# The down projection of twelve inner tiles as a 2x2 block product, with its operands formed in the gate and up phase

## The chip, the cores and the metric

The kernel runs on one core of a Trainium2 chip. That core has a matrix engine (TensorE, PE in the profile), a vector engine (VectorE, DVE), a scalar engine (ScalarE, ACT), GpSimd (POOL), and SyncE (SP), whose queue issues all transfers of this kernel. The metric is the device time of one execution in microseconds.

## The reference

One encoder layer on 1024 tokens of width 1024, in float32: a feed-forward half step, a mixer, a second feed-forward half step, each followed by a layer norm.

```python
def swiglu_ffn(x, w_gate, w_up, w_down):
    return (jax.nn.silu(x @ w_gate) * (x @ w_up)) @ w_down
...
    x = layer_norm(ALPHA * x + 0.5 * swiglu_ffn(x, ffn1_w_gate[l], ffn1_w_up[l], ffn1_w_down[l]), ln1_g[l], ln1_b[l])
    x = layer_norm(ALPHA * x + hybrid_mixer(x, w_in[l], na_rpb[l], ...), ln2_g[l], ln2_b[l])
    x = layer_norm(ALPHA * x + 0.5 * swiglu_ffn(x, ffn2_w_gate[l], ffn2_w_up[l], ffn2_w_down[l]), ln3_g[l], ln3_b[l])
```

The inner width of the feed-forward is 2816 = 22 tiles of 128. The mixer is not touched by the change.

## The kernel before

**Layout.** Activations are held transposed: a tile is 128 features by 512 tokens, so an activation of width 1024 is 8 tiles `d` by 2 halves `h` of the tokens. Every float32 matrix product is three passes over a pair of rounded parts: with a = ah + al and b = bh + bl it is ah·bh + ah·bl + al·bh (`mm_steps`, L108). So each tile that feeds a product exists as a pair, high and low, made by `split` (L123): a copy on ScalarE rounds, a subtraction on VectorE leaves the rest. Weights are loaded whole and split the same way in `load_w` (L94).

**Stages of a feed-forward** (class `Ffn`, L412; method `go`, L613). Two inner tiles are formed plainly (`glu`, L448). The other twenty are formed in `blocks` (L511): gate and up of a tile, over the two halves of the input features and the two halves of the tokens, are a 2x2 block product, done in seven products of four feature tiles each instead of eight (Winograd's form of Strassen). `factors` (L472) forms the seven weight factors on VectorE and ScalarE, `sums_of` (L430) the four sums of the input, `product` (L499) runs one product of 12 matmuls. The products of one tile are interleaved with the last two of the tile before: `s3` and `a22` of the previous tile stand between those of the present one. At the end a last round has only those two. Each inner tile is written to DRAM (`hid`, L535 and L550).

Then comes down: `down_block` (L600) reads tiles 0 to 5 and then 6 to 11 back (`fetch`, L592), splits them, and adds their product with the down weights, for each `d` and `h`, into an accumulator `acc[d][h]` (L573) that starts as 2·ALPHA·x + product (L567, L569). The last ten tiles are done half by half (`finish`, L576): all `d` of the first 512 tokens, then all `d` of the second. The layer norm of a half (`Norm`, L197) runs beside the matmuls of what follows. In the second feed-forward the second half is cut into two parts of 256 tokens; the last one is normed token by token (`TokenNorm`, L321) into a different output.

**What sets the order.** PE runs its instructions in the order in which they are written. The other engines and SP's queue get their order from a planner that simulates the program; `high_priority(offset=HOIST)` lets an instruction come up to 100 places early. Within one tag of a pool the slots are handed out in the order of the program. The steps of a norm are placed by a clock of estimated matmul time: `at(delay, fn)` (L176) puts `shift`, `stats`, `scale` and `apply` some units after the step before (`LAGS_A` and the like), one unit being about one microsecond; a `gap` spaces the eight `apply` steps. The transposes and spreading matmuls of the norm stand at those places in PE's order. After the first feed-forward, `tok_major` (L674) is the first reader of the normed activation, first of its first 512 tokens.

**Memory.** `xpool` has 32 slots for the pairs of the current activation, `apool` 16 for the accumulators and residuals, the feed-forward's own pool 14 pairs `hh`/`hl`, four `sr` and seven `hr`, and `wpool` two raw weight buffers and four pairs `wh`/`wl`, open for the whole kernel. PSUM has four banks for products (`dps`, L120).

Of the kernel before, what the change touches and what calls it, by code (L numbers as in the profile page):

```python
# [24 lines left out]
BLOCKS = ((0, 6), (6, 6))  # L25
LAST = ((12, 6), (18, 4))
# [13 lines left out]
LAGS_A = (5.0, 9.5, 8.0, 2.0)  # L40
LAGS_B = (2.6, 5.5, 4.7, 1.3)
# [15 lines left out]
def hybrid_layer(ctx, tc, xT, wg1, wu1, wd1, wg2, wu2, wd2, wcol, wnv, wgv, wdl, wgate,  # L57
# [3 lines left out]
    ln_lags = {(0, 0): (LAGS_A, 2.0), (0, 1): (LAGS_B, 0.0),  # L61
# [13 lines left out]
    wpool = pool(ctx, "wpool", 4)  # L75
# [4 lines left out]
    dram = pool(ctx, "dram", 1, DRAM)  # L80

# [12 lines left out]
    def load_w(src, n, resident=False, ahead=HOIST):  # L94
        raw = wpool.tile([P, n], F32, tag="raw", name=nm("raw"), bufs=2)
        if resident:
            wh, wl = xpool.tile([P, n], F32R, tag="x", name=nm("wh")), \
                xpool.tile([P, n], F32R, tag="x", name=nm("wl"))
        else:
            wh = wpool.tile([P, n], F32R, tag="wh", name=nm("wh"))  # L100
            wl = wpool.tile([P, n], F32R, tag="wl", name=nm("wl"))
# [49 lines left out]
    raw = wpool.tile([P, D], F32, tag="raw", name=nm("raw"), bufs=2)  # L151
    first = [wpool.tile([P, D], F32R, tag=t, name=nm(t)) for t in ("wh", "wl")]
# [259 lines left out]
    class Ffn:  # L412
        def __init__(self, stack, x, xr, hs, wg, wu, wd, idx):
            self.x, self.xr, self.hs, self.wg, self.wu, self.wd = x, xr, hs, wg, wu, wd
            self.idx = idx
            self.hp = pool(stack, "hp", 14)
            self.T = [[None] * 4 for _ in range(4)]
            self.acc = [[None, None] for _ in range(KD)]
            self.ht = [[None, None] for _ in range(FT)]
            self.tmp = tagged(self.hp, ("hr",), 7)  # L420

# [26 lines left out]
        def glu(self, f, ws, h, c0=0, cn=HF, spill=False):  # L448
            cs = slice(c0, c0 + cn)
            rhs = [(a[:, cs], b[:, cs]) for a, b in (self.x[k][h] for k in range(KD))]  # L450
            pg = dps()[:, :cn]
            yield from mm_steps(pg, ws[0], rhs)
            pu = dps()[:, :cn]
            yield from mm_steps(pu, ws[1], rhs)
            with hoist():
                sl = stage()[:, :cn]
                nc.scalar.activation(sl, pg, AF.Silu)
                hr = self.tmp()[:, :cn]
                nc.vector.tensor_tensor(hr, pu, sl, ALU.mult)
            if spill:  # L460
                nc.sync.dma_start(self.hs[f, :, h * HF:(h + 1) * HF], hr)
                return
# [762 lines left out]
```

## Time and profile before

| | us |
|---|---|
| runs: median (lowest to highest) of 3 | 2195.89 (2193.54 to 2195.95) |
| the profiled execution, its own time | 2196.31 |
| its span in the trace | 2194.5 |
| first feed-forward: down starts | 435.6 |
| first feed-forward: last ten tiles, first half | 566.1 to 620.5 |
| first feed-forward: last ten tiles, second half | 620.5 to 685.5 |
| second feed-forward: down starts | 1920.0 |
| second feed-forward: last ten tiles, two parts of the second half | 2105 to 2181 |

A time of a stage is read on PE's timeline, from the span's start. The duration of a matmul in a row is longer than the time it costs, since matmuls overlap; the distance between the starts of two of them is what PE pays. A group of instructions by line can be that of a helper (L115 to L117, L124, L125), so shapes and tile names tell what is meant: `hh`, `hl` are a pair of an inner tile or a factor, `xh`, `xl` of the activation, `wh`, `wl` of weights, `hr` a staging tile, `d` a bank of PSUM.

### The profile page before, as it was taken

Reading aid. Unit: us, or ns where it says so; the run is one execution under the profiler, and the core shown is the slowest. Engines: PE = TensorE matmul, PEld = TensorE weight load, DVE = VectorE, ACT = ScalarE, POOL = GpSimd, SP = SyncE. Lnnn points to the kernel's source line nnn. Section 1 sums busy time; section 2 is a strip of 40 time slices with the busy share of each in tenths; the row PEclk is TensorE's granted clock in tenths of the full one; section 3 lists DMA queues with packets and bytes.
Section 4 is the critical chain, followed back from the end, with each engine's and each line's share of the span. In section 5 each row is a group of like instructions: output and inputs, shape, how many; then the busy total and the mean of one; then the engine's idle time right before and its main releaser. Section 6 shows DMA issues by size and latency. Waiting matters only on the chain.

```text
span 2194.5 us, 26421 instructions
## 1 busy us (share of the span) xinstructions
PE 2155.8 (98%) x10160; PEld 1749.6 (80%) x10160; DVE 1249.0 (57%) x2076; ACT 869.6 (40%) x1379; POOL 99.0 (5%) x96
## 2 busy tenths in 40 slices
PE   9999999999999999999999999999999999999987
PEld 7888888888878867777777788877888888888877
DVE  7655555454567354545667533599755555454467
ACT  6433333321334344446566522245533333322334
POOL 0000000000014000000000000043000000000011
PEclk9999999999999999999999999999999999999989
DMA  5222222333332322223332222321322222333333
GB/s 170 91 85 79 82 87 87 113 117 103 98 94 81 112 77 85 86 70 110 101 92 78 92 78 86 92 86 44 103 80 87 87 86 75 112 121 110 112 112 113
DMA packets 97278, 207.01 MB, mean 94 GB/s; under 512 B 10144, under 2 KB 27296, under 8 KB 97152
## 3 DMA queue, kind: packets, MB, share of 16 engines
q1 hardware_dynamic: 97152, 205.32, 29.4%
q8 instruction: 80, 1.31, 0.2%
q14 instruction: 46, 0.38, 0.1%
HBM read 165.31 MB, written 39.98 MB: 94 GB/s over the span
## 4 chain that ended last, share of the span: by engine, by line
PE 87%; DVE 8%; ACT 2%; issue 1%; DMA 1%; POOL 0%; SPq 0%; DVEq 0%; ACTq 0%
PE d L505 11%; PE d L507 11%; PE d L506 11%; PE d L115 11%; PE d L117 11%; PE d L116 11%; PE d L584 3%; PE d L583 3%; PE d L585 3%; PE d L684 1%; PE d L686 1%; PE d L685 1%; PE po L829 1%; PE pt L811 1%; PE s L794 1%
## 5 line engine op out<-in xcount | busy, mean ns | idle before, releaser
L104 ACT ACTIVATE wh<-raw 128x768 fp32r<-128x768 f32 (+2 forms) x167 | 147.3, 884 | 366.0 <-PE d L116 242.4
L115 PE MATMUL d<-xh,wh 128*128 128x512 f32 x640 | 260.0, 406 | 0.2
L116 PE MATMUL d<-xl,wh 128*128 128x512 f32 x640 | 251.1, 392 | 1.0 <-POOL xl L393 0.5
L117 PE MATMUL d<-xh,wl 128*128 128x512 f32 x640 | 251.2, 392 | 0.5 <-DVE wl L105 0.5
L105 DVE TENSOR_TENSOR wl<-raw,wh 128x768 fp32r<-128x768 f32 (+2 forms) x167 | 170.2, 1021 | 136.3 <-ACT wh L104 135.6
L124 ACT ACTIVATE hh<-sr 128x512 fp32r<-128x512 f32 x136 | 86.0, 632 | 254.6 <-DVE sr L486 145.7
L583 PE MATMUL d<-hh,wh 128*128 128x512 f32 (+1 forms) x400 | 144.0, 360 | 8.6 <-ACT hh L124 8.6
L115 PE MATMUL d<-hh,wh 128*128 128x512 f32 x384 | 149.4, 389 | 0.0
L116 PE MATMUL d<-hl,wh 128*128 128x512 f32 x384 | 149.4, 389 | 0.0
L117 PE MATMUL d<-hh,wl 128*128 128x512 f32 x384 | 149.4, 389 | 0.0
L115 PEld LDWEIGHTS d<-xh,wh 128*128 128x128 f32 x640 | 120.4, 188 | 34.6 <-issue 5.5
L584 PE MATMUL d<-hl,wh 128*128 128x512 f32 (+1 forms) x400 | 142.6, 356 | 1.5 <-DVE hl L125 1.3
L117 PEld LDWEIGHTS d<-xh,wl 128*128 128x128 f32 x640 | 120.5, 188 | 27.3 <-DVE wl L105 1.0
L585 PE MATMUL d<-hh,wl 128*128 128x512 f32 (+1 forms) x400 | 141.3, 353 | 0.0
L116 PEld LDWEIGHTS d<-xl,wh 128*128 128x128 f32 x640 | 120.7, 189 | 25.7 <-DVE xl L125 1.1
L505 PE MATMUL d<-a,wh 128*128 128x512 f32 x320 | 124.7, 390 | 1.6 <-DVE hr L533 1.6
L506 PE MATMUL d<-a,wh 128*128 128x512 f32 x320 | 124.5, 389 | 0.0
L507 PE MATMUL d<-a,wl 128*128 128x512 f32 x320 | 124.5, 389 | 0.0
L505 PE MATMUL d<-xh,wh 128*128 128x512 f32 x320 | 124.5, 389 | 0.0
L506 PE MATMUL d<-xl,wh 128*128 128x512 f32 x320 | 124.5, 389 | 0.0
L507 PE MATMUL d<-xh,wl 128*128 128x512 f32 x320 | 124.5, 389 | 0.0
L505 PE MATMUL d<-hh,hh 128*128 128x512 f32 x320 | 124.5, 389 | 0.0
(281 smaller groups left out, 4464.1 us busy)
## 6 DMA issues: line engine op xcount, KB each, us to landing
raw<-in_wd SPq DMA_DIRECT2D x72, 384.0 KB
raw<-in_wu SPq DMA_DIRECT2D x44, 512.0 KB
hid<-hr SPq DMA_DIRECT2D x88, 256.0 KB
hr<-hid SPq DMA_DIRECT2D x88, 256.0 KB
raw<-in_wg SPq DMA_DIRECT2D x43, 512.0 KB
raw<-in_wcol SPq DMA_DIRECT2D x16, 512.0 KB
raw<-in_wgate SPq DMA_DIRECT2D x16, 512.0 KB
raw<-in_wout SPq DMA_DIRECT2D x16, 512.0 KB
```

Of the source, the lines that this page charges most:

```text
L104: nc.scalar.activation(wh, raw, AF.Copy)
L105: nc.vector.tensor_tensor(wl, raw, wh.bitcast(F32), ALU.subtract)
L115: nc.tensor.matmul(ps, a, xh, start=k == 0, stop=False)
L116: nc.tensor.matmul(ps, a, xl, start=False, stop=False)
L117: nc.tensor.matmul(ps, wl[:, k * m:(k + 1) * m], xh, start=False, stop=k == n - 1)
L124: nc.scalar.activation(hi, src, AF.Copy)
L505: nc.tensor.matmul(ps, a, xh, start=first and k == 0, stop=False, **sg)
L506: nc.tensor.matmul(ps, a, xl, start=False, stop=False, **sg)
L507: nc.tensor.matmul(ps, wl[:, k * P:(k + 1) * P], xh, start=False, stop=k == 3, **sg)
L583: nc.tensor.matmul(ps, a, hi[:, cs], start=j == 0, stop=False)
L584: nc.tensor.matmul(ps, a, lo[:, cs], start=False, stop=False)
L585: nc.tensor.matmul(ps, wl[:, i * P:(i + 1) * P], hi[:, cs], start=False, stop=j == len(todo) - 1)
```

## The change

Of the 22 inner tiles, 2 to 13 are taken in six pairs. For each pair (the two halves of the inner features), each two output tiles `2m`, `2m+1` and the two halves of the tokens, down becomes a 2x2 block product in seven products of three pairs each (9 matmuls), with the same interleaving as in gate and up. The partial results are added to the accumulators (`gather`) after each product.

The seven operands of a pair are formed when its tiles leave gate and up (`hidden`): four are sums (`t1` to `t4`), all seven are split, and the pairs are written to DRAM (`ops`), through slots of `xpool` whose activation (feature tiles 0 to 3 of the second token half) is no longer needed. Its residual is read again from DRAM when the accumulator starts (`res`; in the second feed-forward it is stored once more as `x2s`). `operands` reads a set of 42 tiles (three pairs), twice per feed-forward; `down_factors` forms the weight factors from a new weight layout `wds`.

Four tiles (0, 1, 14, 15) are done plainly first (`front`) and start the accumulators; six (16 to 21) are done plainly last, half by half, in place of ten. At the end of gate and up the pools of weights and pairs are closed and others opened (`turn`): raw buffers of 1536 elements for 1024, five weight pairs of 768 for four of 1024, five `hr` for seven. `wpool` is no longer open for the whole kernel; the mixer opens its own. `tok_major` keeps its weights in `hh`/`hl` slots. The first norm spaces its eight `apply` steps by 1.0 in place of 2.0.

```diff
-BLOCKS = ((0, 6), (6, 6))
-LAST = ((12, 6), (18, 4))
+PAIRS = 6
+NP = 3
+NF = 4
+REST = (0, 1, *range(2 + 2 * PAIRS, FT))
+FRONT, LAST = REST[:NF], REST[NF:]
...
+GAP_A = 1.0
...
-    ln_lags = {(0, 0): (LAGS_A, 2.0), (0, 1): (LAGS_B, 0.0),
+    ln_lags = {(0, 0): (LAGS_A, GAP_A), (0, 1): (LAGS_B, 0.0),
...
+        def turn(self):
+            self.inner.close()
+            self.wp = pool(self.stack, "wdown", 5)
+            W[:] = self.wp, "w3h", "w3l"
+            self.hp = pool(self.stack, "hq", 14)
+            self.tmp = tagged(self.hp, ("hr",), 5)
...
+        def operand(self, j, i, src):
+            hi, lo = xtile("oh"), xtile("ol")
+            split(src, hi, lo)
+            for n, t in enumerate((hi, lo)):
+                nc.sync.dma_start(self.ops[j, i, n], t.bitcast(F32))
+
+        def hidden(self, f, h, t):
+            j, odd = divmod(f - 2, 2)
+            if j >= PAIRS:
+                nc.sync.dma_start(self.hs[f, :, h * HF:(h + 1) * HF], t)
+                return
+            K = self.keep
+            if not odd and h:
+                K["b12"] = t
+            elif not odd:
+                K["b11"] = t
+                self.operand(j, 0, t)
+                t1 = self.sr()
+                nc.vector.tensor_tensor(t1, K["b12"], t, ALU.subtract)
+                self.operand(j, 3, t1)
+            elif h:
+                self.operand(j, 2, t)
+                t3, t2 = self.sr(), self.tmp()
+                nc.vector.tensor_tensor(t3, t, K["b12"], ALU.subtract)
+                nc.vector.tensor_tensor(t2, t3, K["b11"], ALU.add)
+                self.operand(j, 4, t2)
+                self.operand(j, 5, t3)
+                K["t2"] = t2
+            else:
+                self.operand(j, 1, t)
+                t4 = self.sr()
+                nc.vector.tensor_tensor(t4, t, K["t2"], ALU.subtract)
+                self.operand(j, 6, t4)
...
-                    nc.sync.dma_start(self.hs[g, :, HF:], p2)
+                    self.hidden(g, 1, p2)
...
-                    nc.sync.dma_start(self.hs[g, :, :HF], p1)
+                    self.hidden(g, 0, p1)
...
+        def operands(self, j0):
+            B = [[None] * NP for _ in range(7)]
+            for i in (0, 1, 3, 4, 2, 5, 6):
+                for n in range(NP):
+                    hi, lo = B[i][n] = self.hpair() if i < 3 else (xtile("oh"), xtile("ol"))
+                    for c, t in enumerate((hi, lo)):
+                        nc.sync.dma_start(t.bitcast(F32), self.ops[j0 + n, i, c])
+            return B
+
+        def down_factors(self, j0, m):
...
+            with tc.high_priority(offset=HOIST):
+                nc.sync.dma_start(raw, self.wds[m, :, :, j0 * P:(j0 + NP) * P]
+                                  .rearrange("q p c -> p q c"))
+                flat = raw.rearrange("p q c -> p (q c)")
+                split(flat[:, :2 * n], *ga)
+                s1, s2, s3, s4 = (self.sr()[:, :n] for _ in range(4))
+                nc.vector.tensor_tensor(s1, a21, a22, ALU.add)
+                split(s1, *part(gb, 0))
+                nc.vector.tensor_tensor(s2, s1, a11, ALU.subtract)
+                split(s2, *part(gb, 1))
+                nc.vector.tensor_tensor(s4, a12, s2, ALU.subtract)
+                split(s4, *part(gd, 0))
+                nc.vector.tensor_tensor(s3, a11, a21, ALU.subtract)
+                split(s3, *part(gc, 0))
+                split(a22, *part(gc, 1))
...
+        def plain(self, fs, d, w, h, c0=0, cn=HF):
...
+            yield from mm_steps(ps, w, [(a[:, cs], b[:, cs])
+                                        for a, b in (self.ht[f][h] for f in fs)])
+            if self.acc[d][h] is None:
+                a = self.acc[d][h] = atile()
+                with hoist():
+                    if h and d < 4:
+                        nc.sync.dma_start(a, self.res(d, h))
+                        nc.vector.scalar_tensor_tensor(a, a, 2 * ALPHA, ps, ALU.mult, ALU.add)
+                    else:
...
+            else:
+                self.gather(d, h, ps, cs)
+
+        def gather(self, d, h, ps, cs=slice(0, HF)):
             a = self.acc[d][h][:, cs]
             with hoist():
                 nc.vector.tensor_tensor(a, a, ps, ALU.add)
...
+        def front(self):
+            for h in range(2):
+                for f in FRONT:
+                    self.fetch(f, h)
+            for d in range(0, KD, 2):
+                ws = [load_w(self.wd[e, :, :NF * P], NF * P) for e in (d, d + 1)]
                 for h in range(2):
                     for e, w in enumerate(ws):
-                        run(self.down(b, d + e, w, h))
+                        run(self.plain(FRONT, d + e, w, h))
+
+        def down(self):
+            prev, B = None, None
+            items = [(j0, m) for j0 in range(0, PAIRS, NP) for m in range(4)]
+            for it in [*items, None]:
+                if it:
+                    j0, m = it
+                    B = self.operands(j0) if m == 0 else B
+                    w = self.down_factors(j0, m)
+                    X = dps()
+                    yield from self.product(X, w["a11"], B[0], True)
+                    self.gather(2 * m, 0, X)
+                    Y = dps()
+                    yield from self.product(Y, w["a12"], B[1], True)
+                    self.gather(2 * m, 0, Y)
+                if prev:
+                    pm, pX, pw, pB = prev
+                    yield from self.product(pX, pw["s3"], pB[5])
+                    self.gather(2 * pm + 1, 1, pX)
+                if it:
+                    Z = dps()
+                    yield from self.product(Z, w["s1"], B[3], True)
+                    self.gather(2 * m + 1, 1, Z)
+                    yield from self.product(X, w["s2"], B[4])
+                    self.gather(2 * m, 1, X)
+                if prev:
+                    yield from self.product(pX, pw["a22"], pB[6])
+                    self.gather(2 * pm + 1, 0, pX)
+                if it:
+                    yield from self.product(Z, w["s4"], B[2])
+                    self.gather(2 * m, 1, Z)
+                    prev = m, X, w, B
...
-            for b in range(len(BLOCKS)):
-                self.down_block(b)
-            (f2, n2), (f3, n3) = LAST
-            wr = [None] * KD
+            self.turn()
+            self.front()
+            run(self.down())
...
                 for d in range(KD):
-                    w = load_w(self.wd[d, :, f2 * P:(f2 + n2) * P], n2 * P)
-                    if wr[d] is None:
-                        wr[d] = load_w(self.wd[d, :, f3 * P:(f3 + n3) * P], n3 * P, True)
-                    run(self.finish(d, (w, wr[d]), h, c0, cn))
+                    w = load_w(self.wd[d, :, NF * P:], len(LAST) * P)
+                    run(self.plain(LAST, d, w, h, c0, cn))
                     ln.add(acc[d][h][:, c0:c0 + cn])
```

199 lines of the change are left out of this document (100 added, 99 removed).

## The prediction

> **What bounds the kernel now.** I read the page first: span, busy shares, chain that ended last.
>
> ```profile
> span 2194.5 us, 26421 instructions
> PE 2155.8 (98%) x10160; PEld 1749.6 (80%) x10160; DVE 1249.0 (57%) x2076; ACT 869.6 (40%) x1379; POOL 99.0 (5%) x96
> PE 87%; DVE 8%; ACT 2%; issue 1%; DMA 1%; POOL 0%; SPq 0%; DVEq 0%; ACTq 0%
> ```
>
> PE is busy for 98% of the span and is 87% of the chain, so a matmul that is not issued is time saved, wherever the other engines keep up. Next, the groups by shape for what one instruction lasts:
>
> ```profile
> L115 PE MATMUL d<-hh,wh 128*128 128x512 f32 x384 | 149.4, 389 | 0.0
> L583 PE MATMUL d<-hh,wh 128*128 128x256 f32 x160 | 49.0, 307 | 4.7 <-ACT hh L124 4.7
> L125 DVE TENSOR_TENSOR hl<-sr,hh 128x512 fp32r<-128x512 f32 x136 | 93.1, 687 | 11.5 <-ACT hh L124 9.9
> L105 DVE TENSOR_TENSOR wl<-raw,wh 128x768 fp32r<-128x768 f32 x72 | 69.5, 965 | 38.7 <-ACT wh L104 38.5
> L573 DVE TENSOR_TENSOR a<-a,d 128x512 f32<-128x512 f32 x32 | 22.0, 687 | 72.9 <-PE d L117 72.9
> L124 ACT ACTIVATE hh<-sr 128x512 fp32r<-128x512 f32 x136 | 86.0, 632 | 254.6 <-DVE sr L486 145.7
> ```
>
> 389 ns is not the price of a matmul: they overlap. The price is the distance between starts, in the timeline of PE:
>
> ```profile
> 549.81 0.39 PE L115 MATMUL d<-hh,wh 128*128 128x512 f32 x1
> ...
> 562.50 0.39 PE L117 MATMUL d<-hh,wl 128*128 128x512 f32 x1
> ...
> 2147.36 0.28 PE L584 MATMUL d<-hl,wh 128*128 128x256 f32 x1
> ...
> 2156.84 0.28 PE L585 MATMUL d<-hh,wl 128*128 128x256 f32 x1
> ```
>
> Between the first two lie 56 steps, 12.69/56 = 0.2266 us for 512 columns; between the last two 79 steps, 9.48/79 = 0.1200 us for 256. Last, busy time by stage (columns: length, PE, PEld, DVE, ACT and POOL busy with instruction counts, clock, DMA share, GB/s): the gate and up products; the turn to down; the middle of down; the last ten tiles of each feed-forward by half (first half, then second half of the first one, second half of the second one); the tail.
>
> ```profile
> 110.00:430.00 320.00, 320.00 (x1414) 265.05 (x1413) 169.05 (x243) 112.66 (x182) 0.00 (x0) 1.00 0.26 84
> 430.00:441.00 11.00, 10.21 (x45) 8.10 (x44) 7.82 (x12) 6.28 (x10) 0.00 (x0) 1.00 0.83 274
> 480.00:510.00 30.00, 30.00 (x134) 24.86 (x133) 20.33 (x31) 11.61 (x17) 0.00 (x0) 1.00 0.50 158
> 565.90:620.50 54.60, 54.60 (x242) 45.25 (x241) 27.91 (x38) 15.00 (x21) 5.50 (x4) 1.00 0.30 85
> 620.50:686.00 65.50, 60.73 (x258) 48.12 (x257) 49.67 (x77) 30.12 (x45) 20.59 (x16) 0.97 0.31 99
> 2105.00:2181.00 76.00, 69.32 (x509) 66.24 (x507) 55.06 (x125) 34.44 (x56) 6.96 (x10) 0.91 0.42 134
> 2181.00:2194.50 13.50, 1.47 (x13) 1.14 (x11) 8.51 (x20) 2.38 (x6) 1.73 (x1) 0.65 0.20 78
> ```
>
> VectorE is at 53% in gate and up but at 76% (49.67/65.5) and 72% (55.06/76) in the last halves. That is where a shorter PE meets another engine first.
>
> **The change, part by part.** *Matmuls.* Down of 12 tiles is 12 x 8 x 2 x 3 = 576 matmuls now and 6 pairs x 4 x 7 x 3 = 504 after: 72 fewer per feed-forward, 144 in all, 144 x 0.2266 = 32.6 us. The last pass shrinks from ten tiles to six. In the second feed-forward its second half is cut into 256 columns, so 4 x 8 x 2 x 3 = 192 narrow matmuls (192 x 0.1200 = 23.0) become 96 wide ones in the front (96 x 0.2266 = 21.8): 1.3 us more. PE gain 33.9 us.
>
> *Forming operands in gate and up.* Each pair of tiles adds 4 sums and 7 subtractions on VectorE (11 x 0.69 = 7.6 us), 7 copies on ScalarE (4.4 us) and 14 writes of 256 KB for 4 (2.6 MB more). A pair lasts 2 x 84 x 0.2266 = 38.1 us; VectorE goes from 20.1 (169.05/320 of it) to 27.7 us, 73%, DMA from 84 to some 153 GB/s. It fits on the average. The tight place is the split of the next tile's first factor:
>
> ```profile
> 275.04 1.23 DVE L125 TENSOR_TENSOR wl<-raw,wh 128x1024 fp32r<-128x1024 f32 x1 [0.18 <-ACT wh L124]
> ```
> ```profile
> 277.14 0.39 PE L507 MATMUL d<-xh,wl 128*128 128x512 f32 x1
> ```
>
> It ends at 276.27, its first reader starts at 277.14: 0.9 us of slack. A new subtraction of 0.69 us that slips in front still fits; with a second PE waits about 0.5 us. The operands' writes can stand ahead of the next weights in SP's queue:
>
> ```profile
> 276.29 0.33 SPq L481 DMA_DIRECT2D raw<-in_wg  x1
> ```
>
> Those are split one period later (275.04 + 19.0), and a load takes some 4 to 5 us, so about 12 us are in hand. Cost: 0 to 24 x 0.69 = 16.6 us over both; I take 1.5, near the lower end, since the splits are hoisted and the new work is not.
>
> *Turn of the pools.* The front's tiles lie over old ones and wait for those alone. Of the 7 old slots of `hr`, the last tile holds three, so at least two of the five new ones are free a round earlier and can take the front's reads in turn. From 0 to a late read per feed-forward (4.45 us to landing in the row `620.78` below, plus 0.63 and 0.69 for the split, 5.8 us); I take 1.5 each, 3.0. Behind a late read on SP wait the front's weights.
>
> *Drain of the product pipeline.* In the last round s3 and a22 stand next to each other and share a bank, so PE waits for the vector addition. Gate and up have the same round:
>
> ```profile
> 431.50 0.39 PE L507 MATMUL d<-a,wl 128*128 128x512 f32 x1
> ```
> ```profile
> 432.67 0.50 PE L505 MATMUL d<-a,wh 128*128 128x512 f32 x1 [0.79 <-DVE hr L533]
> 433.01 0.40 PE L506 MATMUL d<-a,wh 128*128 128x512 f32 x1
> ```
>
> 432.67 - 431.50 - 0.23 = 0.94 us, once per feed-forward: 1.9 in all.
>
> *Inside the products of down.* A round is 63 x 0.2266 = 14.3 us. VectorE does 7 gathers (4.8), a 768-wide split (0.97) and nine 384-wide operations (about 0.52 each, an estimate between the 512- and 256-wide rows): 10.5 us, 73%. Each gather has 4 to 5 us before its bank is written again (two 2.04-us products lie between). Weights have five slots for four per round, the tightest with some 8 us to spare. I take 0.
>
> *Operand reads.* One set is 42 reads of 256 KB, two sets per feed-forward. With weights, hidden tiles and residuals the front and the products load 22.0 + 2.1 + 6.3 + 3.7 + 1.0 = 35.1 MB; some 2.1 of it can come earlier into x slots that are free after tile 13. 33.0 MB in 192 x 0.2266 + 504 x 0.2266 = 157.7 us is 209 GB/s, and 274 have been seen (the window 430 to 441). SP issues such reads at this pace:
>
> ```profile
> 428.86 8.10 SPq L597 DMA_DIRECT2D hr<-hid  x9
> ```
>
> 0.90 us each, 37.8 us for a set. The second set finds 9 of its 21 pairs' slots free; the rest come free from 2 us into the last round of the first set, and its last use is two rounds later. Waiting reads hold up the weights queued behind them, which have a round in hand. Cost 0 to 10 us per feed-forward; I take 1.5, together 3.0.
>
> *The last pass.* At the start of its second half PE waits now, and keeps waiting:
>
> ```profile
> 620.53 0.39 PE L585 MATMUL d<-hh,wl 128*128 128x512 f32 x1
> 624.79 0.62 PE L583 MATMUL d<-hh,wh 128*128 128x512 f32 x1 [3.88 <-ACT hh L124]
> 628.25 0.48 PE L584 MATMUL d<-hl,wh 128*128 128x512 f32 x1
> ```
> ```profile
> 619.92 0.33 SPq L103 DMA_DIRECT2D raw<-in_wd  x1
> 620.30 7.96 SPq L597 DMA_DIRECT2D hr<-hid  x10
> ```
> ```profile
> 620.78 4.45 DMA hr<-hid
> ```
>
> The reads of the half stand behind a weight load that waits for its buffer until 619.92; the norm's squares take `hr` slots ahead of them. The new kernel has the same order there, so I leave this wait in. After the wait 7 steps take 3.46 us in place of 1.59: 1.9 us on top of 3.88. Were this paid in proportion, the 7.9 us of small waits above (3.0 + 1.9 + 3.0) would cost 3.9 more, 2184 us. After the 0.94 us of the drain the first step takes 0.34 us and the matmul behind it lasts 0.40 again, so the sum leaves it out. The Trainium skill (TensorE: Matmul & The Clock Gate, Part 1 on the HAM clock gate) has it that way: PE falls to half rate only after an idle window of about 3.4 us. By that rule the sum stays unless one wait is that long.
>
> In the second half VectorE's work stays but for four splits (2.8 us): 46.9 us in the first feed-forward, while PE needs 65.5 - 96 x 0.2266 = 43.7; 52.3 us in the second, where PE needs 76.0 - 23.0 = 53.0. Weights and gathers are hoisted, so what comes late is the norm: the first half's apply, which now has half the gap, then its subtraction on POOL, and the statistics that PE transposes at a fixed place.
>
> ```profile
> 672.46 2.29 POOL L393 TENSOR_TENSOR xl<-a,xh 128x512 fp32r<-128x512 f32 x1 [0.55 <-ACT xh L392]
> ```
> ```profile
> 685.50 0.39 PE L684 MATMUL d<-wh,xh 128*128 128x512 f32 x1
> ```
> ```profile
> 691.79 0.88 PE pl L261 x8
> ```
>
> Now x1 is complete at 674.8, 10.7 us before its reader. After, VectorE is 3.2 us over PE's length in this half and idles about 3 us at its start, so some 6 us of backlog meet a statistics place that comes 5.8 us after the half: 2 to 6 us, I take 4.0. In the second feed-forward 52.3 + 8.5 us of vector work plus the idle time at both ends (3 + 5, from the same windows) is 68.8 us against 53.0 + 13.5 = 66.5 for PE and tail; the narrow part's eight applies now fall due as the tail begins. 2 to 8 us, I take 4.0.
>
> Sum: -33.9 + 1.5 + 3.0 + 1.9 + 0 + 3.0 + 4.0 + 4.0 = -16.5 us. The profiled execution took 2196.3 us (1.8 us around its span), 0.4 above the median of the runs: about 2180 us.
>
> **Rivals.** *All of it is hidden* (0.22): only the drain is paid, -33.9 + 1.9, 2164 us. For it: DVE at 57%, DMA at 29%, most new work far ahead of its use. Against it: the last halves' sums above.
>
> *The last halves are bound by the norm, not by PE* (0.14). They were 65.5 and 76.0 us with DVE idle for 15.8 and 20.9 of them. If those idle times are the norm's own waits, the halves shrink only by the 2.8 us of splits each, while the front still pays for the four tiles: of 21.8 + 23.0 = 44.8 us that PE gives up there 39.2 are not won. -33.9 + 1.9 + 39.2 = +7.2, 2203 us, slower. It decides from 32.0 of the 44.8 us lost. For it: 76% busy. Against it: at least these waits of DVE name PE, and a faster PE shortens them:
>
> ```profile
> 614.15 0.69 DVE L590 TENSOR_TENSOR a<-a,d 128x512 f32<-128x512 f32 x1 [1.06 <-PE d L585]
> ```
>
>
> *Operand reads set the pace* (0.08). 33.0 MB are 126 tiles of 256 KB per feed-forward. At 0.90 us each they need 113 of 157.7 us. Above (157.7 + 16)/126 = 1.38 us a tile the gain is gone; at 1.5 us both feed-forwards lose 31 us each: 2226 us. For it: 158 GB/s, 1.66 us a tile, in the window 480 to 510. Against it: PE did not wait there, and 0.90 is shown where reads are queued. [...]
>
> *A wait at every tile of gate and up* (0.05): 24 x 0.69 = 16.6 us instead of 1.5, 2195 us.
>
> **How the numbers follow.** Forecast 0.51, rivals 0.22, 0.14, 0.08, 0.05. The forecast's own range, with one or two of its small costs at either bound, is 2169 to 2190. For 8 in 10 I reach to the fully hidden case and to the wait in gate and up: 2163 to 2196. This kernel's runs lie within 0.1%; a change under 0.2% (4.4 us) can't be told from none. Faster: forecast 0.50, hidden 0.22, norm-bound but short of the deciding point 0.04, together 0.76. Same: 0.01, 0.05 and 0.05 of the norm's, 0.11. Slower: 0.05 and 0.08, 0.13.
>
> **What would show it.** Right: 9,920 matmuls in place of 10,160 (144 and 96 fewer); starts 0.227 us apart through front and products; one wait near 0.9 us at the end of the products; a second half of about 48 us in the first feed-forward with DVE near full; PE waiting at the half change as now. Wrong: PE waiting on `oh`, `ol` or `hh` with a DMA behind it (reads); many short waits on `wl` in gate and up; no wait at all behind the last halves; last halves still over 60 us.

## The result and the profile after

| | before | after |
|---|---|---|
| runs: median (lowest to highest) of 4, us | 2194.88 (2193.54 to 2195.95) | 2224.49 (2220.21 to 2224.93) |
| the profiled execution, its own time, us | 2196.31 | 2220.21 |
| its span, us | 2194.5 | 2218.4 |

The ratio is 1.0131, 95% interval 1.0113 to 1.0148: the change made the kernel 1.3% slower, where some 0.7% faster was forecast. The profiled execution was the fastest of the four: by the medians the change cost 29.6 us, between the two traces 23.9, and what follows accounts for the 23.9. The page of the kernel after, its span and busy times:

```profile
span 2218.4 us, 26690 instructions
PE 2136.0 (96%) x9920; PEld 1721.4 (78%) x9920; DVE 1386.9 (63%) x2364; ACT 916.0 (41%) x1483; POOL 98.2 (4%) x96
```

The 240 matmuls are gone as planned (10,160 to 9,920), and yet the span rose by 23.9 us. PE got less work and more waits. Where they are shows in the busy times by stage (columns as in the prediction): gate and up; front and products; the last pass of the first feed-forward (first half, half change, second half), the mixer's first product.

```profile
110.00:430.00 320.00, 320.00 (x1414) 264.96 (x1413) 200.04 (x303) 133.42 (x215) 0.00 (x0) 1.00 0.37 129
450.00:600.00 150.00, 150.00 (x664) 124.20 (x663) 105.47 (x178) 36.24 (x65) 0.00 (x0) 1.00 0.62 211
604.00:637.00 33.00, 33.00 (x147) 27.33 (x146) 20.48 (x28) 10.84 (x15) 4.66 (x4) 1.00 0.29 86
637.00:648.00 11.00, 0.92 (x4) 0.48 (x2) 7.83 (x11) 2.62 (x4) 1.35 (x1) 0.72 0.50 145
648.00:690.00 42.00, 38.99 (x162) 30.51 (x161) 32.97 (x60) 18.68 (x31) 8.52 (x9) 0.95 0.32 104
690.00:703.00 13.00, 10.34 (x23) 5.19 (x22) 13.00 (x17) 9.78 (x16) 11.16 (x8) 0.62 0.12 40
```

Where the new work is, in the first two rows, PE does not lose a microsecond: 320 of 320, and 150 of 150 at 211 GB/s. The losses lie at the seams. PE's timeline of the kernel after, around each seam (start, duration, in brackets the idle time and what ended it):

```profile
433.19 0.50 PE L552 MATMUL d<-a,wh 128*128 128x512 f32 x1 [0.78 <-DVE hr L580]
...
435.84 0.39 PE L554 MATMUL d<-a,wl 128*128 128x512 f32 x1
442.87 0.79 PE L118 MATMUL d<-hh,wh 128*128 128x512 f32 x1 [6.64 <-ACT hh L127]
...
600.87 0.39 PE L554 MATMUL d<-oh,w3l 128*128 128x512 f32 x1
602.47 0.47 PE L552 MATMUL d<-oh,w3h 128*128 128x512 f32 x1 [1.21 <-DVE a L665]
...
637.24 0.39 PE L120 MATMUL d<-hh,wl 128*128 128x512 f32 x1
647.71 0.80 PE L118 MATMUL d<-hh,wh 128*128 128x512 f32 x1 [10.08 <-ACT hh L127]
...
689.50 0.67 PE L795 MATMUL d<-hh,xh 128*128 128x512 f32 x1 [3.01 <-ACT xh L398]
...
783.25 0.88 PE L942 MATMUL po<-et,vp 96*64 96x128 f32 x12
...
1502.72 0.79 PE L118 MATMUL d<-xh,wh 128*128 128x512 f32 x1 [5.45 <-ACT wh L107]
...
1932.82 0.50 PE L552 MATMUL d<-a,wh 128*128 128x512 f32 x1 [0.78 <-DVE hr L580]
1942.25 0.79 PE L118 MATMUL d<-hh,wh 128*128 128x512 f32 x1 [6.37 <-ACT hh L127]
2148.39 0.58 PE L118 MATMUL d<-hh,wh 128*128 128x256 f32 x1 [9.90 <-ACT hh L127]
2197.28 1.22 PE L300 MATMUL pl<-sr,ones 128*128 128x256 f32 x2 [6.50 <-DVE a L320]
```

Two landmarks of the kernel before on the same engine, the mixer's first `po` and the drain of gate and up in the second feed-forward:

```profile
771.18 0.88 PE L829 MATMUL po<-et,vp 96*64 96x128 f32 x12
...
1917.10 0.50 PE L505 MATMUL d<-a,wh 128*128 128x512 f32 x1 [0.78 <-DVE hr L533]
```

From landmark to landmark the span splits as follows; the column of matmuls is those saved in that stretch at the prices of the prediction, the rest is waiting.

| stretch | after minus before | of it matmuls | waits |
|---|---|---|---|
| start to the drain of gate and up, first feed-forward (433.19 against 432.67) | +0.5 | 0 | +0.5 |
| to the mixer's `po` (350.06 against 338.51) | +11.6 | -16.3 | +27.9 |
| to the drain in the second feed-forward (1149.57 against 1145.92) | +3.6 | 0 | +3.6 |
| to the end (285.58 against 277.40) | +8.2 | -17.6 | +25.8 |
| sum | +23.9 | -33.9 | +57.8 |

So the gain of 33.9 us is there in full, and 57.8 us of waits stand against it. Adding up, in both traces, by how much each start-to-start distance exceeds that of a stream at full rate, slow steps behind a wait included, gives for the first feed-forward: 9.3 us at the turn (0 before), 1.5 at the end of the products (0 before), 12.6 at the half change (6.8 before), 11.7 at the mixer's first product (0 before, the norm's own matmuls left out in both). For the second: 10.4 at the turn, 1.5, 15.3 at and behind the half change (12.6 before), 12.5 at the end of the last pass (3.5 before), and a tail longer by 2.

The chain that ended last, in order of time, shows what a turn and a half change wait for (start, length, link):

```profile
436.27 0.70 DVE hr L596
436.99 0.32 SPq L520
437.40 0.38 SPq L106
437.88 4.22 DMA hr<-hid
...
641.69 0.88 DVE wl L108
642.59 0.33 SPq L106
642.96 4.04 DMA hr<-hid
```

At the turn, the first read of the front is issued only behind the write of the last inner tile (L520), and that waits for the last multiplication of gate and up (L596). At the half change the reads are issued only behind a weight load, and that waits for a subtraction on VectorE that frees its buffer; the subtraction itself stands behind the norm's operations on VectorE (`sr`, L251 and L248, from 639.80 to 641.69 in the same chain). SyncE's queue shows the same order (start, time taken by the group, waiting included):

```profile
401.25 36.05 SPq L520 DMA_DIRECT2D hid<-hr  x6
...
601.75 41.16 SPq L106 DMA_DIRECT2D raw<-in_wd  x10
642.96 5.76 SPq L713 DMA_DIRECT2D hr<-hid  x6
```

### The profile page after: what moved, and what is told of

The parts are those of the page before. It is cut to its first block, busy times and chain, and to the rows that moved or that the text cites. A ratio compares the mean times of both kernels' runs of the same rounds, so it can differ in the third digit from the quotient of the medians.

```text
span 2218.4 us, 26690 instructions
## 1 busy us (share of the span) xinstructions
PE 2136.0 (96%) x9920; PEld 1721.4 (78%) x9920; DVE 1386.9 (63%) x2364; ACT 916.0 (41%) x1483; POOL 98.2 (4%) x96
## 3 DMA queue, kind: packets, MB, share of 16 engines
q8 instruction: 78, 1.28, 0.2%
## 4 chain that ended last, share of the span: by engine, by line
PE 86%; DVE 7%; ACT 2%; issue 1%; DMA 1%; POOL 1%; SPq 0%; ACTq 0%; DVEq 0%; POOLq 0%
PE d L552 15%; PE d L554 15%; PE d L553 15%; PE d L118 11%; PE d L119 10%; PE d L120 10%; PE d L795 1%; PE po L942 1%; PE d L797 1%; PE pt L924 1%; PE d L796 1%; PE s L907 1%; DVE wl L108 1%; DMA hr<-hid 1%; PE att L1086 1%
## 5 line engine op out<-in xcount | busy, mean ns | idle before, releaser
L107 ACT ACTIVATE wh<-raw 128x1024 fp32r<-128x1024 f32 (+2 forms) x131 | 116.0, 888 | 219.7 <-PE d L119 132.3
L108 DVE TENSOR_TENSOR wl<-raw,wh 128x1024 fp32r<-128x1024 f32 (+2 forms) x131 | 137.4, 1050 | 81.8 <-ACT wh L107 81.6
L665 DVE TENSOR_TENSOR a<-a,d 128x512 f32<-128x512 f32 (+1 forms) x152 | 99.7, 656 | 99.7 <-PE d L554 70.3
L553 PE MATMUL d<-hl,hh 128*128 128x512 f32 x320 | 124.5, 389 | 0.0
L554 PE MATMUL d<-hh,hl 128*128 128x512 f32 x320 | 124.5, 389 | 0.0
L128 DVE TENSOR_TENSOR wl<-raw,wh 128x1024 fp32r<-128x1024 f32 (+2 forms) x84 | 78.0, 928 | 70.9 <-ACT wh L127 70.9
```

What stands on the lines that cost most here:

```text
L107: nc.scalar.activation(wh, raw, AF.Copy)
L108: nc.vector.tensor_tensor(wl, raw, wh.bitcast(F32), ALU.subtract)
L128: nc.vector.tensor_tensor(lo, src, hi.bitcast(F32), ALU.subtract)
L553: nc.tensor.matmul(ps, a, xl, start=False, stop=False, **sg)
L554: nc.tensor.matmul(ps, wl[:, k * P:(k + 1) * P], xh, start=False, stop=k == n - 1, **sg)
L665: nc.vector.tensor_tensor(a, a, ps, ALU.add)
```

## The experiments

The theory after reading the trace: the seams are queueing. Transfers that PE needs next stand in SyncE's queue behind others that wait ("order"), or their target memory is still held ("slots"). The rival: the norms and splits need VectorE's and ScalarE's time whatever the queue does ("norm", "VectorE full"), so that a wait taken away comes back elsewhere. Times are given with the ratio to the kernel before on the same chip. Four chips were used (e1 to e4, e5 to e8, e9 and e10, e11 and e12), and the kernel before took 2194.6, 2195.0, 2196.4 and 2194.7 us on them, so differences of about 2 us between runs of different chips are not read. "Waits at a turn" are counted as above: all that the starts of PE lose, slow steps included.

### The turn: e1, e2, e5

e1:
```diff
             if j >= PAIRS:
-                nc.sync.dma_start(self.hs[f, :, h * HF:(h + 1) * HF], t)
+                q = nc.gpsimd if f == FT - 1 else nc.sync
+                q.dma_start(self.hs[f, :, h * HF:(h + 1) * HF], t)
```


> Edit: the two writes of the last inner tile (21, needed only in the last pass) go through GpSimd's queue, so that nothing on SyncE's queue stands between gate and up and the front's reads and weight loads. Theory 'order': PE's waits at the start of the front (steps of 7.03 and 6.76 us) come from those two writes, which wait for VectorE and stand ahead of the front's first loads. Then both steps fall to 2 us or less and the time falls by some 10 to 16 us against the changed kernel (7 us each with the slow steps behind them): about 2210 us. Rival 'slots': the front's first read lands in memory of a tile of the last round and must wait for it in any queue. Then the steps stay above 5 us and the time stays within 3 us of 2224.

Measured: 2221.51 us, ratio 1.0117 (1.0102 to 1.0132). The queue of SyncE in e1:

```profile
428.25 0.38 SPq L106 DMA_DIRECT2D raw<-in_wd  x1
436.92 0.32 SPq L714 DMA_DIRECT2D hr<-hid  x1
```

The first weight load now leaves 9.2 us earlier, and the first read does not move: its slot lies over one that tile 21 holds until it is written. PE's step is 5.59 us in place of 7.03, but more slow steps follow it: the waits at the two turns are 9.4 and 9.7 us, against 9.3 and 10.4. The runs of the two kernels overlap in time (2220.57 to 2222.20 against 2220.21 to 2224.93). This is what the rival "slots" expected; "order" alone is not the cause.

e2 (`hrp` is opened ahead of the pools that the turn closes; six slots, since seven leave no room for the pool of pairs after the turn):
```diff
+NHR = 6
...
+    H = [pool(ffn1, "hrp")]
...
-            self.tmp = tagged(self.hp, ("hr",), 7)
+            self.tmp = tagged(H[0], ("hr",), NHR)
...
         def turn(self):
...
-            self.tmp = tagged(self.hp, ("hr",), 5)
...
+        H[0] = pool(ffn2, "hrp")
```


> Edit: the staging tiles hr get a pool of their own, of six slots, that is not closed at the turn; all transfers stay on SyncE's queue. In the program the front's eight reads and first two weight loads then stand ahead of the last tile's writes. Theory 'slots' (with 'order' as its consequence: the order of the queue is made by a planner that knows when slots come free): the steps of 7.03 and 6.76 us at the start of the front fall to 2 us or less, 10 to 16 us less in all, about 2210 us. Rival: the front waits for the last tile's data paths themselves (half-rate clock, casts on ScalarE), not for the reads: the steps stay above 5 us. A third way: six slots in place of seven hold up gate and up, seen as waits on hr there; then the time rises.

Measured: 2214.64 us, ratio 1.0087 (1.0072 to 1.0102). Its queue:

```profile
420.41 1.95 SPq L714 DMA_DIRECT2D hr<-hid  x2
...
429.47 6.29 SPq L714 DMA_DIRECT2D hr<-hid  x6
435.81 0.90 SPq L107 DMA_DIRECT2D raw<-in_wd  x2
```

Now the first reads leave at 420.4, 17 us earlier, and it is the weights that come last, behind eight reads of which the later ones wait for six slots. The step is 5.35 us (6.39 in the second feed-forward), not 2 or less as expected; the waits at the two turns are 6.9 and 8.0 us, about 5 less together. Slots alone are a part of the cause. The third way (gate and up held up by six slots) did not happen, the drain stands at 432.89.

e5, on top of e1:
```diff
         def turn(self):
...
             self.tmp = tagged(self.hp, ("hr",), 5)
+            nc.gpsimd.memset(self.tmp()[:, :1], 0.0)
```


> Edit: as e1 (the two writes of tile 21 through GpSimd's queue), and the first slot that the new hr tag hands out is given to a one-column memset, so that the front's first read lands in a slot that no tile of the last round holds. Both causes of the turn are away at once, with seven hr in gate and up as before. Theory 'slots and order together': the first read and the first weight load are issued before 431 us, the steps of 7.03 and 6.76 us fall to 2 us or less, and the time is 12 to 18 us below the changed kernel: 2207 to 2212 us. Rival: the casts of reads and weights on ScalarE and VectorE stand behind the last tile's work in any case; then a step of 4 to 6 us stays, as in e1 and e2, and the time is about 2216.

Measured: 2213.50 us, ratio 1.0076 (1.0057 to 1.0094). Queue and PE of e5:

```profile
427.74 0.38 SPq L106 DMA_DIRECT2D raw<-in_wd  x1
428.17 0.44 SPq L715 DMA_DIRECT2D hr<-hid  x1
```
```profile
435.69 0.39 PE L118 MATMUL d<-hh,wh 128*128 128x512 f32 x1
437.83 0.50 PE L119 MATMUL d<-hl,wh 128*128 128x512 f32 x1 [1.76 <-DVE hl L128]
...
440.86 0.50 PE L119 MATMUL d<-hl,wh 128*128 128x512 f32 x1 [2.05 <-DVE hl L128]
...
442.04 0.63 PE L120 MATMUL d<-hh,wl 128*128 128x512 f32 x1
...
445.03 0.43 PE L118 MATMUL d<-hh,wh 128*128 128x512 f32 x1
```

With both away, weights and first read leave 9.7 us earlier and the front's first matmul follows gate and up without a gap. Two steps of 2.15 and 2.44 us are left (`hl`, the splits of the reads on VectorE), 3.8 us of idle time where e1 and e2 kept 5.2 and 5.0 before the first matmul. The waits at the two turns fall to 6.1 and 6.0 us, 7.6 us less together. The median is 11.0 us below the changed kernel's, short of the 12 to 18 expected; more than the 7.6 is not shown at the turns. So "slots and order together" is shown for some 40% of the waits, and 6 us per turn stay. The two steps left are waits for splits, as the rival had it, though shorter than its 4 to 6 us. For the second step the trace names memory once more: the split stands on VectorE behind a weight subtraction at 439.51 that waits 1.73 us for a write of `hid`.

### The half change: e3, e4

e3:
```diff
-            for h, c0, cn in parts:
-                if c0 == 0:
-                    for f in LAST:
-                        self.fetch(f, h)
+            for h in range(2):
+                for f in LAST:
+                    self.fetch(f, h)
+            for h, c0, cn in parts:
```


> Edit: the six tiles of the second half are read and split before the first half of the last pass begins, not at the half change. Theory 'order': the steps of 10.47 and 10.28 us at the two half changes go away and with them the slow steps behind them, about 12 us per feed-forward; what is won stays won apart from a few us at the norm: 2204 us or less. Rival 'norm': the first half's norm (VectorE, ScalarE, GpSimd) needs its time in any case, and PE meets it where the mixer reads x1 (10 us of waits there now) and at the end of the second feed-forward: the waits there grow by what the half change gives, and the time stays within 6 us of 2224.

Measured: 2198.89 us, ratio 1.0014 (1.0003 to 1.0024): 25.6 us less than the changed kernel, within 0.2% of the kernel before. Busy times of e3 in the first feed-forward's last pass:

```profile
637.00:669.00 32.00, 32.00 (x143) 25.82 (x142) 28.04 (x50) 15.28 (x25) 9.21 (x9) 1.00 0.35 103
669.00:690.00 21.00, 13.89 (x43) 8.19 (x42) 21.00 (x30) 12.25 (x19) 11.76 (x9) 0.84 0.23 74
```

The wait is gone whole and is not given back. That is more than the change had added: of the 27.9 us of waits at the two half changes (12.6 and 15.3), 19.4 stood in the kernel before too (6.8 and 12.6). The half now takes what its matmuls take. Behind it VectorE is full (21.00 of 21.00) and PE still waits for `xh` and `xl`, about as long as before: the first such step is 3.40 us here and was 3.40 us in the changed kernel. "Order" holds for the half change, in the sense that the place of the reads made the wait; what held the queue there was VectorE. "Norm" is left for the seam after it.

e4 has the edits of e2 and e3.

> Edits of e2 and e3 together: hr in a pool of its own across the turn, both halves' reads ahead of the last pass. If both causes are as 'slots' and 'order' say and do not share their gains, the time is the changed kernel's less both gains: about 2224 - 14 - 20 = 2190 us, near the kernel before. If the norm binds the last pass, it is about 2224 - 14 - 4 = 2206.

Measured: 2192.04 us, ratio 0.9987 (0.9978 to 0.9996). The gains add within the spread of the runs: 9.9 and 25.6 are 35.5, and 32.5 came.

### The second feed-forward's end and its start: e6, e7

e6, on top of e3 and e5:
```diff
-GAP_3A = 2.0
+GAP_3A = 1.0
```

> Edits of e5 and e3 together, and GAP_3A from 2.0 to 1.0. At 2.0 the eight apply steps of the second feed-forward's first half are due 18.9 to 32.9 units after that half, and the second part's spreading matmul, which needs their bank, stands at 28.3 units in PE's order: a step of 6.3 to 6.8 us there in all runs so far. In the kernel before the same matmul stood 10 units later. Theory 'due times': with 1.0 the applies end at 25.9 units, the step falls below 2 us, and the tail loses 4 to 6 us beside what e3 and e5 give (25 and 14): about 2181 us. Rival 'VectorE full': the applies are late because VectorE has no time, and a shorter gap moves nothing: the step stays above 5 us and the time is about 2186.

Measured: 2188.89 us, ratio 0.9966 (0.9953 to 0.9979). The gains of e3 and e5 added up would give 2187.9 (no run has the two together without the gap), so the gap gave nothing. The spreading matmul in e6:

```profile
2164.53 1.22 PE L300 MATMUL pl<-sr,ones 128*128 128x256 f32 x2 [6.75 <-DVE a L320]
```

6.75 us, more than any before. "Due times" falls; the applies are late though due earlier.

e7, on top of e6:
```diff
-    mix.close()
...
-        fa2 = ffn2.enter_context(ExitStack())
-        weights(fa2)
+        fa2 = ffn2.enter_context(mix)
```


> Edit on top of e6: the mixer's weight pool is not closed and reopened but goes over to the second feed-forward. Theory 'the second turn': the step of 5.85 us at the first matmul of the second feed-forward (and the slow ones behind it; 2.05 us before the change) comes from weights that can't be loaded or split ahead, since their memory is new; the step falls to 2 us or less and the time by 3 to 6 us against e6. Rival: ScalarE's cast of these weights stands behind the mixer's last norm whatever memory it has: step and time stay within 1 us.

Measured: 2185.41 us, ratio 0.9942 (0.9924 to 0.9961). The first matmul of the second feed-forward no longer waits. What is left there is the norm's transpose, which took 2.05 us before the change too:

```profile
1495.39 0.66 PE L267 MATMUL pl<-ident,sl 128*128 128x128 f32 x4 [1.66 <-DVE sl L251]
```

### VectorE or the order of the norms: e8, e9, e10, e12

e8, on top of e7:
```diff
-LAGS_B = (2.6, 5.5, 4.7, 1.3)
+LAGS_B = (8.0, 5.5, 4.7, 1.3)
```

> Edit on top of e7: the shift of the first feed-forward's second half comes 8.0 units after its fourth d in place of 2.6, so that the centring and squares of that half don't stand in VectorE's and GpSimd's order between the first half's applies. Theory 'order of the norms': the waits where the mixer's first product reads x1 (3.4 + 1.1 + 1.9 + 1.6 + 1.1 us and half-rate steps, about 10 us) shrink by half or more: 4 to 7 us less than e7. Rival 'VectorE full': the work is only moved behind and the waits move to the second half of the same product: within 2 us of e7, or slower.

Measured: 2184.30 us, ratio 0.9946 (0.9926 to 0.9965): no difference from e7. The waits moved: the step at the mixer's first product grew to 5.34 us, and a spread behind it waits 1.83 us for VectorE. "Order of the norms" falls for this edit.

e9, on top of e7 (the six tiles' weights of one `d` fill three slots of 512 columns):
```diff
+        def keep_w(self, d):
+            raw = self.wp.tile([P, 6 * P], F32, tag="raw", name=nm("raw"), bufs=2)
+            a, b, c = xtile("wa"), xtile("wb"), xtile("wc")
+            n = 4 * P
+            with tc.high_priority(offset=HOIST):
+                nc.sync.dma_start(raw, self.wd[d, :, NF * P:])
+                split(raw[:, :n], a, b)
+                split(raw[:, n:], c[:, :2 * P], c[:, 2 * P:])
...
-                    w = load_w(self.wd[d, :, NF * P:], len(LAST) * P)
+                    w = kept.get(d)
+                    if w is None and d < (8 if idx else 5):
+                        w = kept[d] = self.keep_w(d)
+                    elif w is None:
+                        w = load_w(self.wd[d, :, NF * P:], len(LAST) * P)
```


> Edit on top of e7: in the last pass the weights of the six tiles are loaded and split once and kept in slots of xpool (all eight d in the second feed-forward, five of eight in the first), in place of once per half or part. That takes 16 and 5 of the 0.95-us subtractions from VectorE (15 and 5 us; some 0.16 us are added where a first split falls into two) and as many casts from ScalarE; PE's work, the norms and their due times stay. Theory 'VectorE full': the waits left at the end of the second feed-forward (3.16 and 5.39 us) and at the mixer's first product (8.5 us and half-rate steps) come from VectorE, which is busy for 46 of the 50 us from 2115 to 2165; then the time falls by 8 to 14 us against e7, to 2171 to 2177 us. Rival 'chain of the norm': each step waits for the one before at PE, ScalarE or GpSimd, and less work beside it changes nothing: within 3 us of e7's 2185. A third way: kept weights wait for slots that the products still hold, seen as waits of the last pass's first matmuls; then slower.

Measured: 2169.64 us, ratio 0.9879 (0.9864 to 0.9893): 15.8 us less than e7 (on another chip), and 1.2% below the kernel before. From landmark to landmark 11.9 us of it are won behind the drain of the second feed-forward, and 4.8 between the drain and the mixer's `po` in the first. The page of e9, and its stages in the last pass of the second feed-forward (first half, then most of the two parts):

```profile
PE 2123.2 (98%) x9920; PEld 1715.6 (79%) x9920; DVE 1364.0 (63%) x2356; ACT 900.0 (42%) x1475; POOL 99.2 (5%) x102
```
```profile
2077.00:2110.00 33.00, 33.00 (x146) 27.30 (x147) 15.79 (x25) 5.51 (x11) 5.07 (x4) 1.00 0.14 43
2110.00:2127.00 17.00, 17.00 (x137) 16.65 (x136) 12.11 (x32) 3.38 (x6) 2.62 (x5) 1.00 0.01 1
2127.00:2144.00 17.00, 17.00 (x134) 16.04 (x133) 15.29 (x41) 6.45 (x13) 2.99 (x4) 1.00 0.13 47
```

PE is full in all three stretches, and the wait at the spreading matmul, 5.11 us in e7, is 0.26 us. The edit takes away casts on ScalarE and loads along with the subtractions, so by itself it does not tell which of them kept the norm late. The busy times of e7 where the norm is late do:

```profile
2115.00:2165.00 50.00, 41.78 (x306) 39.54 (x305) 46.32 (x102) 22.96 (x36) 8.80 (x11) 0.91 0.38 119
```

VectorE is busy for 46.32 of the 50 us, ScalarE for 22.96, and the DMA engines for 38%. At this seam it was VectorE's work; its average of 63% over the span says nothing of it. At the mixer's first product the relief did less: some 10 us of waits are left there (13.8 in e7, 11.7 in the changed kernel).

e10 has the edits of e9 and e8.

> Edits of e9 and e8's (the shift of the first feed-forward's second half 8.0 units after its fourth d). In e8 the waits only moved (5.3 us at the first x1 in place of 3.4, 2.2 at a spread). If VectorE was the reason, it has room now and the late shift lets the first half's applies through: 2 to 5 us less than e9. If the order of the norms is not what x1 waits for: within 2 us of e9.

Measured: 2171.49 us, ratio 0.9891 (0.9875 to 0.9908): 1.9 us above e9, where 2 to 5 less would have spoken for the order of the norms. With fewer weight splits on VectorE the late shift still helps nothing.

e12 is e9 with `GAP_3A` at 2.0.

> Edit: e9 with GAP_3A back at 2.0. With VectorE relieved, theory 'due times' (e6) can be told apart from 'VectorE full': at 2.0 the last applies are due at 32.9 units, the second part's spreading matmul, which needs their bank, stands at 28.3; if due times bind now, a step of 3 us or more comes back at that matmul and the time rises by 2 to 6 us against e9's 2169.6. If the planner runs the applies as early as VectorE allows in any case: within 1.5 us of e9.

Measured: 2169.64 us, ratio 0.9881 (0.9865 to 0.9897): the gap is worth nothing in time either way. The step at the spreading matmul is 1.87 us, against 0.54 in e9, less than the 3 us that "due times" asked for.

### The price of the matmuls: e11

e11, on top of e9:
```diff
                     yield from self.product(X, w["a11"], B[0], True)
+                    yield from self.product(X, w["a11"], B[0], True)
```


> Edit on top of e9: the first of the seven products of each round of down is run twice into the same bank (the second run overwrites the first), 9 matmuls more per round, 16 rounds: exactly the 144 matmuls that the change saves, with nothing else added. Theory 'PE pays each matmul in full there': 144 x 0.2266 = 32.6 us more than e9, about 2202 us. Rival 'the products are paced by reads of operands or by VectorE's factors': part of the added time is hidden; under 25 us more.

Measured: 2203.67 us, ratio 1.0039 (1.0026 to 1.0053), 34.0 us above e9. The page of e11:

```profile
PE 2155.3 (98%) x10064; PEld 1741.9 (79%) x10064; DVE 1366.8 (62%) x2356; ACT 900.9 (41%) x1475; POOL 99.4 (5%) x102
```

144 matmuls more cost 34.0 us (as much against e12, which ran on the same chip), 0.236 us each, against 0.2266 from the starts; the 1.4 us between the two lie within the spread of the runs. Nothing of them is hidden.

## Why the prediction was wrong

The forecast was -16.5 us and the traces differ by +23.9, so 40.4 us were missed. By term: turns 16.7 too little, the norm in the last halves 14.7, the half changes 8.5, the pool behind the mixer 3.6, the drains 1.1; forming operands was 1.0 too much and operand reads 3.0. These add up to 40.6.

*Matmuls* (-33.9): right. e11 prices the 144 at 34.0 us, where 32.6 were taken.

*Forming operands in gate and up* (+1.5): too careful. The first drain row comes 0.5 us later, but PE is two matmuls behind already at 17 us, ahead of the first pair; from 110 to 430 PE is full, with VectorE at 63% (200.04 of 320). *Inside the products* (0) and *operand reads* (+3.0): right or too careful; PE lost nothing from 450 to 600 with 211 GB/s moving, where 209 was worked out. So the rivals "operand reads set the pace" and "a wait at every tile" are out. Of the change's own arithmetic and traffic nothing was mis-priced by more than 3 us.

*Drain of the products* (0.94 each): mechanism right, size 1.60 - 0.23 = 1.37 us.

*Turn of the pools* (1.5 each, at most 5.8): wrong, 9.3 and 10.4 us, the largest error. The step that failed is "at least two of the five new ones are free a round earlier and can take the front's reads in turn". Such slots existed, but the first one handed out was not one of them (e1: the read waits though the queue is free), and everything on the queue stands behind the write of tile 21 (with either cause left, e1 and e2, a step of 5.35 us or more stays). With both away (e5) the waits are 12.1 us in place of 19.7; where the rest comes from is not shown. The bound was wrong too: it held one late read, not a queue that starts only after the last multiplication, and no slow steps, though the granted clock is 0.72 in the row of the wait at the half change (637 to 648) and 0.62 at the mixer's first product (690 to 703). The Trainium skill (TensorE: Matmul & The Clock Gate, Part 1 on the HAM clock gate) ties this to an idle window of about 3.4 us, and the prediction let the sum stand "unless one wait is that long". Six were (5.45 us and more in the timeline above), and there the trace agrees: behind each, starts stand 0.43 us apart for 512 columns, or 0.21 for 256, before they return to the full rate. At the mixer's first product the same follows a wait of 3.01 us and smaller ones.

*The last pass* ("I leave this wait in"): wrong, by 5.8 and 2.7 us. The order of the queue was indeed the same. But the wait is what remains of the reads' delay after the half in front of it has run. That half shrank from 54.6 to 32.9 us, and the reads, behind weight loads that wait for VectorE, left only 16 us earlier (54.2 us after the half's first matmul before, 38.4 now). Step 4.27 became 10.47 us (4.41 became 10.28). That it was no fixed cost at all, e3 shows: 25.6 us come back with the reads moved ahead of the pass, those of the kernel before included.

*Norm in the last halves* (+4.0 and +4.0, at most 6 and 8): sizes short at both places, and the mechanism, VectorE's backlog, shown at one. At the mixer's first product the waits are 11.7 us (0 before), at the second feed-forward's end 12.5 us (3.5 before) with 2 us more tail. VectorE was taken at its average over the half; in the stretch where the norm needs it, it is full (13.00 of 13.00 from 690). For the second feed-forward's end e7's busy times and e9 confirm it: 11.9 us come back there with 16 of 21 weight splits gone, and the due times are out (e6, e12). For the mixer's first product it is shown in small part only: e9 takes 3.5 us off e7's 13.8, some 10 stay, and the order of the norms changes nothing (e8, e10). There GpSimd is busy for 11.16 of the 13 us too.

*Not in the prediction*: the mixer's weight pool now closes ahead of the second feed-forward. +3.6 us in that stretch, and e7 brings back 3.5. The turn was thought of, and the same close two stages later was not.

The second half of about 48 us was forecast and came (637.24 to 685.65), by chance: 10.1 us of it are a wait that was left at 3.9, and part of the norm had moved behind it. The rival "last halves bound by the norm" had the sign and a part of the mechanism, with 2203 us; the turn and the longer half change, 9.3 + 12.6 - 6.8 = 15.1 us in the first feed-forward alone, were in no rival.

What stays open: in e9 PE still loses some 6 us per turn, 4 of them idle, and some 10 us at the mixer's first product, 4 of them idle. No edit here told whether the copies on ScalarE, the subtractions on GpSimd (`xl`) or VectorE end those; the rows name all three. At the mixer's first product GpSimd is a rival that no run tested. In the changed kernel one `xl` takes 1.28 us there, while PE comes to the next after three matmuls, 0.68 us:

```profile
695.19 1.28 POOL L399 TENSOR_TENSOR xl<-a,xh 128x512 fp32r<-128x512 f32 x1 [0.17 <-ACT xh L398]
```

## What to carry to other kernels

When a stage in front of a wait gets shorter, the wait gets longer, unless what it waits for moves as far: here the half became 22 us shorter, the reads came 16 us earlier, and the step grew by 6. Take a stall at a boundary as a distance between two chains, never as a constant. Where pools are closed and reopened, ask for each first transfer which slot it is given, who holds that memory last, and what stands ahead of it in its queue; with the queue alone put right (e1) 19.1 of the 19.7 us of waits stayed, with both put right 12.1. And read an engine's share in the stretch that the shorter engine leaves, not over the span: VectorE at 63% was the bound at the end of the second feed-forward, and taking repeated weight loads and splits away was worth nearly half of what the whole change saves on PE.

## What the runs showed of the hardware

Two short waits can cost PE its full rate. In e5 the waits of 1.76 and 2.05 us end 3 us apart with three matmuls between them, neither is 3.4 us long, and yet the starts from 442.04 to 445.03 stand 0.43 us apart, half rate, before 0.23 returns. The Trainium skill (TensorE: Matmul & The Clock Gate, Part 1 on the HAM clock gate) puts the loss after at least one idle window of about 3.4 us, and says that the window runs freely; the stretch of half rate is about one such window long, but here PE was not idle through any. In e9, at the mixer's first product, no wait is longer than 0.98 us, and starts from 675.08 to 676.79 and from 685.49 to 687.20 stand 0.43 us apart as well:

```profile
673.13 0.50 PE L815 MATMUL d<-hh,xh 128*128 128x512 f32 x1 [0.98 <-ACT xh L399]
...
675.51 0.63 PE L816 MATMUL d<-hl,xh 128*128 128x512 f32 x1
675.93 0.63 PE L817 MATMUL d<-hh,xl 128*128 128x512 f32 x1
```

So small waits that follow each other are not free, against what the prediction took from the drain.
